# Two transformer blocks on one core: small identity products of another width and type

## The chip, the cores and the metric

The kernel runs on one core of one Trainium2 chip. The metric is the device time of one execution in microseconds; a median over runs is given, and one execution is profiled.

## The reference

Two blocks work on 256 tokens of 1024 features in fp32. The first has chunked attention beside a gated linear recurrence and a feed-forward layer; the second has four feed-forward layers, a spatial gating unit and stick-breaking attention. Each of these stages starts with a normalisation by the tokens' root mean square, and is nearly all matrix products. Cut to what matters here:

```python
def rms_norm(x, g):
    y = xf * lax.rsqrt(jnp.mean(xf * xf, axis=-1, keepdims=True) + NORM_EPS)
    return (y * g.astype(jnp.float32)).astype(x.dtype)

def swiglu(h, w_in, w_out):
    gu = h @ w_in
    gate, up = jnp.split(gu, 2, axis=-1)
    return (jax.nn.silu(gate) * up) @ w_out

def second_block(...):
    for i in range(DEPTH_2):
        x = x + FFN_RES_SCALE * swiglu(rms_norm(x, ffn_norm[i, 0]), ...)
        h = rms_norm(x, mix_norm[i])
        x = x + (chunked_sgu(h, ...) if i < N_A else stick_breaking_attention(...) @ b_w_o[j])
        x = x + FFN_RES_SCALE * swiglu(rms_norm(x, ffn_norm[i, 1]), ...)
    return rms_norm(x, final_norm)
```

## The kernel before

The program is one straight line of instructions in the order in which the code is written; each engine works off its own queue, and nothing is reordered by a planner at run time. Activations lie with features on the 128 partitions and the 256 tokens along the free axis.

**The large products.** A weight block of 1024 columns by 128 rows arrives by DMA into `raw`. ScalarE copies it to `h`, rounded to TensorE's fp32r format, and VectorE subtracts to get the remainder `l` (`prep`). The activations are split in the same way into `xh` and `xl` (or `rr`, `rr`). `mm3` makes each product from three: `h` with `xh`, `h` with `xl`, `l` with `xh`. All go through the helper `mm`, line 211, so every product in the trace has the line L211; it is told apart by the names of its tiles. Most have a weight block of 128x128 and 256 columns; a few stages (`pe_nat`, `pe_rn`) have 512 columns. fp32 and fp32r products load their own weights; a bf16 one has a separate weight load, which the order below shows as LDWEIGHTS.

**The stages.** Block 1: the columns of `w_in`, the recurrence's gates, attention, `w_o`. Then `ffn("f0")`, `ffn("f1")`, the gating unit (`sgu`), `ffn("f2")`, `ffn("f3")`, the keys and values, stick-breaking attention (`stick`), `ffn("f4")`. In a feed-forward stage the first groups of columns run on activations that aren't normalised yet; `ffn_order` then mixes groups of columns ("G") with groups of rows of the second matrix ("R").

**The normalising factors.** `stats_a` sums the squares over the partitions with two fp32 products of one column (`ones`), and GpSimd makes the factor of each token, in `rc`. `stats_b` spreads the factors over the partitions with two fp32 products of `rc` with the identity (`bcast_mm`, in the trace `ident,rc`), and ScalarE copies the result to `R`. Between the two, `nudge` issues one more product: a bf16 identity of 64 rows (`identb`) with 32 of its own columns, into a place of the bank that nobody reads.

**Where such products stand.** Sixteen in all: eight in `stats_b` (block 1, f0, f1, the gating unit, f2, f3, `stick`, f4); one behind the second broadcast of f1 (`sbb` in `block2`, line 876); one in the gating unit behind the last of `mix` (line 1066); six by `due`. `due` is set where a G group with i == 5 begins (line 772), so that `pe_a` issues the product ahead of that group's first large product, into the same place, which the large product then overwrites; this happens once in each of the five feed-forward stages, and once in block 1 behind the recurrence's last gate products (line 659).

Of the kernel before, what the change touches and what calls it, by code (L numbers as in the profile page):

```python
# [106 lines left out]
class Builder:  # L107
    def __init__(self, tc, dram, pools):
        self.tc, self.nc, self.dram = tc, tc.nc, dram
        self.cp, self.rawp, self.hlp, self.accp, self.wkp = pools  # L110
        self.ci = 0
        self.preps = 0
        self.loads = 0
        self.raw = {}
        self.hl = {}
        self.gens = []
        self.R = None
        self.rcol = None
        self.due = False

    @property
    def gi(self):
# [106 lines left out]
    def pe_a(self, h, l, xs, out, first):  # L229
        XH, XL = xs  # L230
        if first and self.due:
            self.nudge(out[:, 0:32], True)
            self.due = False
        for k in range(8):
            s = slice(k * 128, k * 128 + 128)
            self.mm3(out, h[:, s], l[:, s], XH[:, k, :], XL[:, k, :], start=(first and k == 0), stop=(k == 7))
# [52 lines left out]
            self.mm(bank[:, half, t * 128:(t + 1) * 128], col[:, t:t + 1].to_broadcast([128, 128]), self.ident,  # L289
                    start and t == 0, True)  # L290

    def nudge(self, out, start=False):

        self.mm(out, self.identb[0:64, :], self.identb[0:64, 0:32], start, True)

    def stats_a(self, pool=None, kv=False):

# [7 lines left out]
    def stats_b(self):  # L305

        self.bcast_mm(self.st, 1, self.rcol, False)
        self.nudge(self.st[:, 0, 64:96])
        self.nc.scalar.activation(self.R, self.st[:, 1, :], AF.Copy)

    def Rpair(self):
# [302 lines left out]
    def lru(self, xr, xc, rt, it, gr, gb, ga, gw):  # L614
# [4 lines left out]
        def conv(k):  # L619
            nc.scalar.activation(xc[:, k, :], xr[:, k, 0:256], AF.Identity, bias=P("conv_b", k), scale=P("conv_w", k))  # L620
            for j in range(1, 4):
                nc.vector.scalar_tensor_tensor(xc[:, k, :], xr[:, k, j:j + 256], P("conv_w", 8 * j + k), xc[:, k, :],
                                               op0=ALU.mult, op1=ALU.add)
# [30 lines left out]
        for p in range(4):  # L654
            banks = [self.acc(), self.acc()]
            for wi in range(2):
                for f in range(2):
                    self.mm(banks[wi][:, f, :], gw[:, wi * 8 + 2 * p + f, :], xc[:, 2 * p + f, :], f == 0, True)
            self.due = p == 3
            if p < 2:  # L660
                conv(2 * p + 4)
            yield
            for f in range(2):
                k = 2 * p + f
                nc.scalar.activation(rt[:, k, :], banks[0][:, f, :], AF.Sigmoid, bias=P("b_r", k))
            yield
            if p < 2:
                conv(2 * p + 5)
            yield
            for f in range(2):  # L670
                k = 2 * p + f
                nc.scalar.activation(it[:, k, :], banks[1][:, f, :], AF.Tanh, bias=self.half[:, k:k + 1], scale=0.5)
            yield
            sl = slice(2 * p, 2 * p + 2)
            nc.vector.scalar_tensor_tensor(it[:, sl, :], it[:, sl, :], 1.0, xc[:, sl, :], op0=ALU.add, op1=ALU.mult)
# [683 lines left out]
```

## Time and profile before

| what | value |
|---|---|
| median of 3 runs | 1422.33 us (1422.17 to 1423.14) |
| profiled execution, its own time | 1422.0 us |
| its span | 1420.3 us |
| TensorE (PE) busy | 1410.6 us, 99% |
| VectorE (DVE) busy | 949.8 us, 67% |
| ScalarE (ACT) busy | 735.0 us, 52% |
| granted TensorE clock, mean | 0.999 |

The span runs from the first to the last instruction; the execution's own time has 1.7 us more around it. Busy time of TensorE overlaps in the records: a product starts before the one ahead of it has ended, so the rate at which products follow is read from their starts, or from a window's length and the count in it, and not from their durations. A window of the profile lists the engine's busy time and, behind an x, the instructions that touch it; a timeline row gives start, duration, instruction, out<-in, rows\*columns of the array, and the operand's shape.

### The profile page before, as it was taken

The page shows a single profiled execution, that of the slowest core. Times are in us where ns is not written, and L with a number is a line of the kernel's source. Part 1 is how long each engine was busy: PE and PEld are TensorE (multiplying, and loading weights), DVE is VectorE, ACT ScalarE, POOL GpSimd, SP SyncE. Part 2 cuts the span into 40 slices and gives each one's busy share as a digit, 9 for nine tenths or more (in the row PEclk, how much of TensorE's full clock was granted, in tenths as well). Part 3 has the DMA queues.
Part 4 walks back from the last instruction along what each step waited for, and adds up shares of the span by engine and source line. Part 5 has one row for each costly group of instructions (what it writes and reads, how often), then busy time and mean ns, then how long its engine had stood idle before and what let it go on. Part 6 is the DMA issues. An engine that isn't in the chain of part 4 may idle for free.

```text
span 1420.3 us, 26991 instructions
## 1 busy us (share of the span) xinstructions
PE 1410.6 (99%) x11564; PEld 1368.7 (96%) x11564; DVE 949.8 (67%) x1316; ACT 735.0 (52%) x1094; POOL 24.7 (2%) x57
## 2 busy tenths in 40 slices
PE   9999999999999999999999999999999999999998
PEld 9998999999999999998999999999999998999997
DVE  6976687665567666677785665667665677656663
ACT  5686465544445445455445444446544477544442
POOL 0000000000000000000000000000000000000000
PEclk9999999999999999999999999999999999999999
DMA  8555554555544555556445554454555552445551
GB/s 299 192 198 197 176 189 154 203 195 191 179 178 149 206 182 206 203 198 223 160 156 183 186 206 179 178 188 169 208 184 211 199 179 90 161 152 197 190 187 51
DMA packets 37624, 260.31 MB, mean 183 GB/s; under 512 B 4224, under 2 KB 4608, under 8 KB 7040
## 3 DMA queue, kind: packets, MB, share of 16 engines
q1 hardware_dynamic: 36288, 253.77, 50.1%
q0 software_dynamic: 1072, 4.72, 1.0%
q8 instruction: 90, 1.47, 0.4%
q14 instruction: 30, 0.25, 0.1%
q10 hardware_dynamic: 144, 0.10, 0.0%
HBM read 257.53 MB, written 1.05 MB: 182 GB/s over the span
## 4 chain that ended last, share of the span: by engine, by line
PE 98%; DMA 0%; ACT 0%; DVE 0%; SPq 0%; issue 0%; POOLq 0%; POOL 0%
PE wk L211 62%; PE acc L211 36%; DMA raw<-w 0%; PE acc L530 0%; PE wk L530 0%; ACT sf L971 0%; ACT sd L961 0%; DVE l L164 0%; ACT h L163 0%; SPq L361 0%; SPq L352 0%; DVE sf L962 0%; POOLq L1355 0%; POOL rc L284 0%; ACT sh L1148 0%
## 5 line engine op out<-in xcount | busy, mean ns | idle before, releaser
L164 DVE TENSOR_TENSOR l<-raw,h 128x1024 fp32r<-128x1024 f32 (+1 forms) x479 | 571.3, 1220 | 241.3 <-ACT h L163 240.9
L211 PE MATMUL wk<-xh,h 128*128 128x256 f32 x2272 | 637.5, 281 | 1.4 <-ACT h L163 1.4
L211 PE MATMUL wk<-xh,l 128*128 128x256 f32 x2272 | 633.5, 279 | 0.1
L211 PE MATMUL wk<-xl,h 128*128 128x256 f32 x2272 | 633.2, 279 | 0.0
L163 ACT ACTIVATE h<-raw 128x1024 fp32r<-128x1024 f32 (+1 forms) x479 | 486.3, 1046 | 61.3 <-PE acc L211 28.0
L211 PEld LDWEIGHTS wk<-xh,h 128*128 128x128 f32 x2272 | 430.8, 190 | 4.5 <-issue 2.0
L211 PEld LDWEIGHTS wk<-xh,l 128*128 128x128 f32 x2272 | 427.7, 188 | 0.5 <-DVE l L164 0.5
L211 PEld LDWEIGHTS wk<-xl,h 128*128 128x128 f32 x2272 | 427.6, 188 | 0.5
L211 PE MATMUL acc<-rr,h 128*128 128x256 f32 x2016 | 353.5, 279 | 0.0
L211 PEld LDWEIGHTS acc<-rr,h 128*128 128x128 f32 x2016 | 306.1, 189 | 2.1 <-issue 1.9
L211 PE MATMUL acc<-rr,l 128*128 128x256 f32 x1008 | 280.4, 278 | 0.0
L211 PEld LDWEIGHTS acc<-rr,l 128*128 128x128 f32 x1008 | 189.3, 188 | 0.0
L748 ACT ACTIVATE sa<-sa 128x256 f32<-128x256 f32 x110 | 45.4, 417 | 258.5 <-DVE sa L315 258.3
L318 ACT ACTIVATE rr<-sa 128x256 fp32r<-128x256 f32 (+1 forms) x122 | 52.7, 439 | 185.3 <-DVE sa L753 128.9
L315 DVE TENSOR_TENSOR sa<-wk,rt 128x512 f32<-128x512 f32 x92 | 62.4, 687 | 72.5 <-PE wk L211 54.8
L319 DVE TENSOR_TENSOR rr<-sa,rr 128x256 fp32r<-128x256 f32 (+1 forms) x122 | 54.1, 451 | 53.4 <-ACT rr L318 53.4
L211 PE MATMUL acc<-h,rr 128*128 128x512 f32 (+1 forms) x208 | 63.1, 374 | 0.0
L211 PEld LDWEIGHTS acc<-h,rr 128*128 128x128 f32 x208 | 38.5, 188 | 6.6
L262 ACT ACTIVATE xh<-x,par 128x256 fp32r<-128x256 f32 x56 | 25.0, 501 | 29.4 <-DVE x L325 16.2
L211 PE MATMUL acc<-l,rr 128*128 128x512 f32 (+1 forms) x104 | 39.0, 375 | 0.0
L753 DVE TENSOR_TENSOR sa<-sa 128x256 f32<-128x256 f32 x88 | 37.1, 429 | 0.0
L211 PE MATMUL wk<-rr,h 128*128 128x256 f32 x192 | 33.0, 277 | 0.0
(255 smaller groups left out, 972.8 us busy)
## 6 DMA issues: line engine op xcount, KB each, us to landing
raw<-w SPq DMA_DIRECT2D x237, 1024.0 KB, 5.0
sd<-bias POOLq DMA_DIRECT2D x8, 384.0 KB, 3.4
raw<-w SPq DMA_DIRECT2D x3, 512.0 KB, 7.6
sh<-gates SPq DMA_DIRECT2D x1, 1024.0 KB, 9.1
out<-sf SPq DMA_DIRECT2D x4, 256.0 KB, 2.2
x<-x SPq DMA_DIRECT2D x3, 256.0 KB, 6.6
raw<-w SPq DMA_DIRECT2D x2, 256.0 KB, 4.9
sa<-ws POOLq DMA_DIRECT2D x1, 512.0 KB, 3.8
```

The source lines that it names most:

```text
L163: nc.scalar.activation(h[:, s], raw[:, s], AF.Copy)
L164: nc.vector.tensor_tensor(l[:, s], raw[:, s], h[:, s].bitcast(F32), op=ALU.subtract)
L211: self.nc.tensor.matmul(out, lhsT, rhs, start=start, stop=stop, skip_group_check=True)
L262: self.nc.scalar.activation(xs[0][:, k, :], src[p][:, f, :], AF.Copy, scale=self.par(*g(k)))
L315: self.nc.vector.tensor_tensor(dst, bank, self.Rpair(), op=ALU.mult)
L318: self.nc.scalar.activation(zh, src, AF.Copy)
L319: self.nc.vector.tensor_tensor(zl, src, zh.bitcast(F32), op=ALU.subtract)
L748: nc.scalar.activation(t[:, 0, :], t[:, 0, :], AF.Silu)
L753: nc.vector.tensor_tensor(t[:, 1, :], t[:, 0, :], t[:, 1, :], op=ALU.mult)
```

## The change

`nudge` takes its width from the place that it is given, and has a second form. In the eight calls of `stats_b` the bf16 product has 38 columns instead of 32. Where `due` is 2, which is the one place behind the recurrence's last gates, the product is made with the fp32 identity `ident` (64 rows, 32 columns) instead of `identb`. The other products of the kind keep their 32 columns and bf16: the five of the feed-forward stages, the one of the gating unit's `mix` and the one behind f1's second broadcast.

```diff
         XH, XL = xs
         if first and self.due:
-            self.nudge(out[:, 0:32], True)
-            self.due = False
+            self.nudge(out[:, 0:32], True, self.due == 2)
+            self.due = 0
...
-    def nudge(self, out, start=False):
-
-        self.mm(out, self.identb[0:64, :], self.identb[0:64, 0:32], start, True)
+    def nudge(self, out, start=False, wide=False):
+
+        e = self.ident if wide else self.identb
+        self.mm(out, e[0:64, :], e[0:64, 0:out.shape[-1]], start, True)
...
         self.bcast_mm(self.st, 1, self.rcol, False)
-        self.nudge(self.st[:, 0, 64:96])
+        self.nudge(self.st[:, 0, 64:102])
...
-            self.due = p == 3
+            self.due = 2 if p == 3 else 0
```

TensorE's order at the first of the eight broadcasts, before (-) and now (+); `acc` and `wk` are banks of PSUM, `xh`, `xl`, `h` the operands of the large products:

```order
 L211 MATMUL acc<-ident,rc 128x128 x2
 L211 LDWEIGHTS identb
-L211 MATMUL acc<-identb 128x32
+L211 MATMUL acc<-identb 128x38
 L211 MATMUL wk<-xh,h 128x256
 L211 MATMUL wk<-xl,h 128x256
```

Nothing moves; one product is six columns wider, and the large products follow it as before. TensorE's order behind the recurrence's last gates, at the first product of the next group of columns:

```order
 L211 MATMUL wk<-xl,h 128x256
 L211 MATMUL wk<-xh,l 128x256
-L211 LDWEIGHTS identb
-L211 MATMUL wk<-identb 128x32
+L211 MATMUL wk<-ident 128x32
 L211 MATMUL wk<-xh,h 128x256
 L211 MATMUL wk<-xl,h 128x256
```

Here the separate weight load is gone, since an fp32 product loads its own; the product stands at the same place.

## Rows read from the trace of the kernel before

**Rows 1.** The page: TensorE's busy time, and the chain that ended last, by engine.

```profile
PE 1410.6 (99%) x11564; PEld 1368.7 (96%) x11564; DVE 949.8 (67%) x1316; ACT 735.0 (52%) x1094; POOL 24.7 (2%) x57
...
PE 98%; DMA 0%; ACT 0%; DVE 0%; SPq 0%; issue 0%; POOLq 0%; POOL 0%
```

**Rows 2.** Windows of long stretches (f0, f1, f2, f3): length, PE busy (count), clock, DMA.

```profile
294.95:461.83 166.88, 166.88 (x1418) 1.00 0.51 182
483.64:630.64 147.00, 147.00 (x1298) 1.00 0.59 212
808.29:975.16 166.87, 166.87 (x1417) 1.00 0.53 191
995.86:1154.02 158.16, 158.16 (x1393) 1.00 0.55 194
```

**Rows 3.** Groups of large products within f0, then within f1: busy, mean ns.

```profile
L211 PE MATMUL wk<-xh,h 128*128 128x256 f32 x310 | 87.2, 281 | 0.0
...
L211 PE MATMUL wk<-xh,h 128*128 128x256 f32 x272 | 75.2, 276 | 0.0
```

**Rows 4.** Windows of block 1 (first stretch; behind the gates) and of f4.

```profile
29.38:46.45 17.07, 17.07 (x145) 1.00 0.34 120
73.17:107.19 34.02, 34.02 (x289) 1.00 0.55 193
107.19:129.59 22.40, 22.40 (x98) 1.00 0.50 170
1247.76:1256.35 8.59, 8.59 (x73) 1.00 0.31 96
...
1276.66:1282.15 5.49, 5.49 (x26) 1.00 0.58 191
```

**Rows 5.** Timeline of TensorE around the small products of f0 and f4.

```profile
294.62 0.28 PE L211 MATMUL acc<-rr,l 128*128 128x256 f32 x1
294.83 0.19 PE L211 MATMUL wk<-identb 64*128 64x32 bf16 x1
294.95 0.38 PE L211 MATMUL wk<-xh,h 128*128 128x256 f32 x1
295.17 0.28 PE L211 MATMUL wk<-xl,h 128*128 128x256 f32 x1
...
1265.21 0.39 PE L211 MATMUL acc<-h,rr 128*128 128x512 f32 x1
1265.53 0.19 PE L211 MATMUL wk<-identb 64*128 64x32 bf16 x1
1265.65 0.39 PE L211 MATMUL wk<-xh,h 128*128 128x256 f32 x1
```

**Rows 6.** The first large product behind the broadcast: in f0, in f3.

```profile
L211 PE MATMUL wk<-xh,h 128*128 128x256 f32 x1 | 0.4, 388 | 0.0
...
L211 PE MATMUL wk<-xh,h 128*128 128x256 f32 x1 | 0.4, 384 | 0.0
```

**Rows 7.** Timeline of TensorE: the sums ahead of f0, f1's two broadcasts.

```profile
273.62 0.28 PE L211 MATMUL wk<-xh,l 128*128 128x256 f32 x1
273.74 0.50 PE L211 MATMUL acc<-ones,sb 128*128 128x1 f32 x4
274.10 0.36 PE L211 MATMUL wk<-xh,h 128*128 128x256 f32 x1
274.30 0.28 PE L211 MATMUL wk<-xl,h 128*128 128x256 f32 x1
...
468.82 0.19 PE L211 MATMUL acc<-identb 64*128 64x32 bf16 x1
468.94 0.71 PE L211 MATMUL acc<-ident,r1c 128*128 128x128 f32 x4
469.58 0.19 PE L211 MATMUL acc<-identb 64*128 64x32 bf16 x1
469.69 0.39 PE L211 MATMUL wk<-xh,h 128*128 128x256 f32 x1
```

More of the change, by code (lines that the diff above doesn't have):

```diff
@@ L231, in pe_a @@
         if first and self.due:
-            self.nudge(out[:, 0:32], True)
-            self.due = False
+            self.nudge(out[:, 0:32], True, self.due == 2)
+            self.due = 0
         for k in range(8):
```

## The prediction

> **What bounds the kernel now.** I read the page's busy line and its chain first: TensorE is busy 99% of the span and 98% of the chain that ended last is TensorE [rows 1]. Nothing is waited for, so only what TensorE's own products take can change the time. Next I read the windows by stretch, looking at stretches with nothing in them but large products (128x256, three to each weight block). There the reader is to see that the same instructions run at two rates. In the first feed-forward f0, 1416 products take 166.88 us; in f1, 1296 products take 147.00 us [rows 2] (the count of a row includes one or two instructions that began before its window). That is 117.85 ns and 113.43 ns for a product, **4.42 ns** apart, at the same granted clock of 1.00, the 2.4 GHz level, in both. So it isn't the clock. The mean duration tells the rates apart too: 281 ns in f0, 276 ns in f1 [rows 3]. I call them the loose and the tight rhythm. f2 is loose like f0 (166.87 us), f3 is tight like f1 (158.16 us for 1392) [rows 2]. Products of 512 columns have the same pair: 22.40 us for 96 is 233.3 ns, 5.49 us for 24 is 228.8 ns [rows 4].
>
> A rhythm hardly ever changes inside such a stretch; it is set where something else passes. Three products take 340 ns in the tight rhythm and 353.3 ns in the loose one; both are whole multiples of 6.67 ns (51 and 53). Taken to the nanosecond, which the trace keeps and the printed rows round to ten, all starts of tight stretches lie at one place of a raster of 6.67 ns that runs through the whole span, and those of loose stretches at three, a third of the raster apart. So I take the rhythm to be settled by **where in the raster the first large product behind an interruption starts**; I call that its place, counted in ns from where tight stretches start theirs.
>
> **What the change does, part by part.** Eight small products get 38 columns for 32. The first question is whether that moves anything. Around such a product TensorE doesn't overlap: the small one starts 0.21 us after the last 256-column product and 0.32 us after the last 512-column one, and the next large one 0.12 us after the small one [rows 5]. So 256 more columns cost 0.11 us (0.43 ns each), and from 32 to 256 columns the step grows by 0.09 us (0.40 ns each): it is a fixed part of about 0.10 us and a stream of some 0.41 ns a column. Six more columns then start the next product **2.5 ns later**. As work that is 8 x 2.5 ns = 0.02 us, no gain and no loss; as a place in the raster it is three eighths of a period. The ends of this term are 0 (the width is hidden behind a fixed part) and 6 x 0.43 = 2.6 ns; I take 2.5, since the steps behind 32, 256 and 512 columns lie on one line.
>
> The Trainium skill, "TensorE: Matmul & The Clock Gate", section "Back-to-back issue gap", lists one and the same spacing for anything from 1 to 64 columns. By that rule 32 and 38 columns would be alike and these eight edits would do nothing; no row here shows a bf16 product of another width under 64 columns, so it isn't excluded. It is the second rival.
>
> The places, worked out from the starts to the nanosecond. At six of the eight broadcasts a large product follows at once. It starts at 3.4 in four of them (first stretch of block 1, f0, f2, f4), and all four turn loose; at 1.2 in f3 and 0.6 in the stick-breaking stage, and both turn tight. In f1 and in the gating unit another small product follows. That the four are one case shows in the rows: the first large product lasts 388 ns at each of the four, 384 ns in f3 [rows 6]. Behind the other small products, which don't change, places 0.1 to 0.5 led to the loose rhythm, 3.9 to 4.2 and 6.0 to the tight one; behind the value products of the attention, whose 64 columns also make TensorE wait, 5.7 to 6.1 led to the tight one each time. So places 0.1 to 0.5 and about 2.9 to 3.4 lead into the loose rhythm, all others that were seen into the tight one. The change puts the four from 3.4 to **5.9**: tight.
>
> That settles most of it. Behind the broadcast in f0 come 120 products and then the small one that `due` sets, which keeps 32 columns: from a tight stretch it led into a tight one in f1 and f3, from a loose one into a loose one in f0 and f2. So f0 gains on 120 + 1416 = 1536 products: 1536 x 4.42 ns = 6.79 us. f2 has the same counts: 6.79 us. Block 1's 144 products [rows 4] give 144 x 4.42 = 0.64 us, f4's 72 give 0.32 us.
>
> f3 is tight now only because it comes out of a loose f2: its places are shifted against f0's from the start. With f2 tight it enters as f0 does now, its broadcast at 3.4 + 2.5 = 5.9 too: tight again, 0 us. f1 has two broadcasts in a row, the first now with 38 columns and the second still with 32 [rows 7], and it too comes out of a tight stretch for the first time; carried through its steps its entry falls near 6.1 or 4.7, both tight, so 0 us, but this is the least certain step. The gating unit is tight behind its broadcast; two rounds of small products stand between, so I leave it so (0 us; at worst 132 wide and 144 large products turn loose, +1.2 us). The stick-breaking stage moves from 0.6 to 3.1, loose, for 36 products until other work interrupts: +0.16 us. Two brief stretches (48 at the gates, 24 in f1) should turn loose, since what comes before them is tight: 72 x 4.42 = +0.32 us.
>
> The product at the gates becomes fp32: its separate weight load goes, and it makes more than one pass. Bound from below: two fp32 products of one column, without a change of rows, put 0.68 us between the starts of the large products around them [rows 7], where two plain steps would take 0.23; so 0.22 us each. The bf16 one now costs 0.32 (0.21, 0.12 and 0.22 to the second large product [rows 5], less the 0.23 of two plain steps), by 0.10 more: -0.10 us. From above: the fp32 broadcast behind a 64-row product takes 0.21 us from its first half to its second (0.64 us to the next small product, less two halves of 0.11 and a wait of 0.21) [rows 7], all of it extra: +0.21 us. It has 64 rows as well, so I lean to the upper end: +0.1. What it does to the rhythm counts more. The 288 products and 96 wide ones behind it are loose now [rows 4]. The places it can reach spread over most of the raster, of which about two thirds are tight; I take tight: 288 x 4.42 = 1.27 and 96 x 4.5 = 0.43, together 1.70 us.
>
> Sum: -6.79 - 6.79 - 0.64 - 0.32 - 1.70 + 0.16 + 0.32 + 0.10 + 0.02 = **-15.6 us**. The profiled execution took 1422.0 us, so 1406.4; the median of the runs is 0.3 us higher, so **1406.8 us**. Covers: TensorE in f0 and f2 would want its weights 4% earlier, and f1 and f3, with the same plan, already run so without a wait.
>
> **The rivals.**
> 1. f1 tips. Its second broadcast lands in a loose place, and with it the whole of f1: 1416 x 4.42 = 6.3 us given back: 1413.1. For it: two small products in a row, and an order of entry that the trace doesn't hold. Against it: both ways of carrying the steps through end in tight places.
> 2. The width is hidden, and only the gates' product acts: -1.6 us if it gives the tight rhythm, +0.1 if not: 1420.7 to 1422.4. For it speaks that the step behind the small product can't be seen at another width; against it the line through 32, 256 and 512 columns.
> 3. Slower. The width moves the entry by 2.5 ns, but 5.9 is a loose place for these. Then f0 and f2 stay loose, f3 still comes out of a loose f2, and its entry goes from 1.2 to 3.7, which lies between 3.4 (loose) and 3.9 (tight). If that is loose, f3's 120 + 1392 products lose 1512 x 4.42 = 6.7 us: 1427 to 1429. It decides from a place of under about 3.65. Against it: every entry seen between 5.7 and 6.1 turned tight.
> 4. As rival 3, but f3 stays tight: about 1421.
>
> **How the numbers follow.** Forecast 0.47 (1405 to 1409, by whether the gates turn tight), rival 1 0.16, rival 2 0.20, rival 3 0.11, rival 4 0.06. A measurement of this kernel can tell about 0.2% (2.8 us) from no change. Faster by more: 0.47 + 0.16 = 0.63; within it: 0.20 + 0.06 = 0.26; slower: 0.11. The range runs from 1405.0 to 1422.6, which leaves out rival 3 and the tails of the others; the forecast's own range is 1405 to 1409.
>
> **What would show it.** In the changed kernel's trace: the step from the small product to the next large one at the broadcasts stays 0.12 us, but the mean duration of f0's and f2's large products falls from 281 to 276 ns, and their main stretches take about 160.6 us; f1's and f3's stay at 276 ns. If f0 still shows 281 ns while the first large product behind its broadcast lasts other than 388 ns, the width moved the entry and I had the wrong map; if it still lasts 388 ns, the width is hidden. If f1 or f3 shows 281 ns, rival 1 or 3. The forecast is wrong as a whole if the rhythm isn't settled at these entries, which would show as changes of rhythm in the middle of a stretch.

## The result, and the profile after

The changed kernel takes 1407.41 us (1407.05 to 1407.65 in 4 runs), the kernel before 1422.74 us beside it (1422.17 to 1424.44 in 4 runs): a ratio of 0.9892, with a 95% interval from 0.9877 to 0.9907, so 15.3 us less. The forecast of 1406.8 us was 0.6 us off. The profiled execution took 1407.16 us, its span 1405.4 us against 1420.3 us.

The page's line on busy time, and the chain by engine, answer to [rows 1]:

```profile
PE 1395.3 (99%) x11565; PEld 1353.6 (96%) x11565; DVE 949.4 (68%) x1316; ACT 735.0 (52%) x1094; POOL 24.8 (2%) x57
...
PE 98%; DMA 1%; ACT 0%; SPq 0%; DVE 0%; issue 0%; POOLq 0%; POOL 0%
```

TensorE has one instruction more, is as full as before, and is done 15 us earlier. VectorE and ScalarE do the same work in the same time. So the products follow one another more closely, and the windows of the stretches say where. Columns: window and its length, PE busy (instructions that touch it), granted clock, DMA share, GB/s. In this order: block 1's first stretch, behind the gates (256-wide and 512-wide), the main stretches of f0, f1, f2, f3, the stick-breaking stage's, f4's:

```profile
29.99:46.44 16.45, 16.45 (x145) 1.00 0.32 121
73.56:106.33 32.77, 32.77 (x289) 1.00 0.58 198
106.33:128.30 21.97, 21.97 (x98) 1.00 0.52 174
293.15:453.75 160.60, 160.60 (x1417) 1.00 0.53 190
475.66:622.66 147.00, 147.00 (x1297) 1.00 0.59 212
799.79:960.39 160.60, 160.60 (x1417) 1.00 0.55 198
981.09:1139.25 158.16, 158.16 (x1393) 1.00 0.54 194
...
1144.60:1149.04 4.44, 4.44 (x37) 1.00 0.64 240
...
1233.22:1241.50 8.28, 8.28 (x73) 1.00 0.28 83
```

Against [rows 2, 4]: f0 and f2 went from 166.88 and 166.87 to 160.60 us each, the same 1416 products at the same clock; f1 (147.00) and f3 (158.16) are where they were. The 120 products ahead of f0's main stretch, first in the kernel before, then in the changed one:

```profile
280.49:294.83 14.34, 14.34 (x121) 1.00 0.27 89
```

```profile
279.21:293.03 13.82, 13.82 (x121) 1.00 0.27 82
```

The groups of products within f0's main stretch and, under the dots, the product behind its broadcast (busy us, mean ns) answer to [rows 3] and [rows 6]:

```profile
L211 PE MATMUL wk<-xh,h 128*128 128x256 f32 x312 | 86.2, 276 | 0.0
...
L211 PE MATMUL wk<-xh,h 128*128 128x256 f32 x1 | 0.4, 394 | 0.0
```

f0 now has the mean of 276 ns that f1 had, and its first large product lasts 394 ns, which neither the 388 of the old f0 nor the 384 of f3 is: it starts at another place in the raster. The timeline of TensorE at the two kinds of changed product (start, duration, instruction, rows\*columns, operand), at f0's broadcast and at the gates:

```profile
278.56 0.61 PE L211 MATMUL acc<-ident,rc 128*128 128x128 f32 x4
279.09 0.19 PE L211 MATMUL acc<-identb 64*128 64x38 bf16 x1
279.21 0.39 PE L211 MATMUL wk<-xh,h 128*128 128x256 f32 x1
...
73.02 0.28 PE L211 MATMUL wk<-xh,l 128*128 128x256 f32 x1
73.23 0.41 PE L211 MATMUL wk<-ident 64*128 64x32 f32 x2
73.56 0.39 PE L211 MATMUL wk<-xh,h 128*128 128x256 f32 x1
```

The step behind the 38-column product is still 0.12 us. The fp32 one is two passes, and lies 0.54 us between the large products around it where the bf16 one took 0.33 (0.21 and 0.12 in [rows 5]).

Places in the raster are worked out from starts to the nanosecond, finer than the rows print; those below were found as the prediction's were. The starts of the tight stretches drift against an exact 6.67 ns by about 1.6 ns in a millisecond, which is taken out, and a start is a whole nanosecond, so a place is good to about half a nanosecond. In the changed kernel the entries of block 1, f0, f1, f2, f3 and f4 stand at 5.9, 6.3, 5.9, 6.1, 5.4 and 6.1, all tight; the stick-breaking stage's at 3.0, loose; the one at the gates at 2.6, tight.

### The profile page after: what moved, and what is told of

Its sections match the earlier page's. It is cut to its first block, busy times and chain, and to the rows that moved or that the text cites. A ratio compares the mean times of both kernels' runs of the same rounds, so it can differ in the third digit from the quotient of the medians.

```text
span 1405.4 us, 26993 instructions
## 1 busy us (share of the span) xinstructions
PE 1395.3 (99%) x11565; PEld 1353.6 (96%) x11565; DVE 949.4 (68%) x1316; ACT 735.0 (52%) x1094; POOL 24.8 (2%) x57
## 3 DMA queue, kind: packets, MB, share of 16 engines
q8 instruction: 90, 1.47, 0.4%
## 4 chain that ended last, share of the span: by engine, by line
PE 98%; DMA 1%; ACT 0%; SPq 0%; DVE 0%; issue 0%; POOLq 0%; POOL 0%
PE wk L211 62%; PE acc L211 36%; DMA raw<-w 1%; PE acc L531 0%; PE wk L531 0%; ACT sf L972 0%; ACT sd L962 0%; SPq L362 0%; DVE l L164 0%; ACT h L163 0%; SPq L351 0%; SPq L353 0%; DVE sf L963 0%; POOLq L1356 0%; POOL rc L284 0%
## 5 line engine op out<-in xcount | busy, mean ns | idle before, releaser
L211 PE MATMUL acc<-rr,h 128*128 128x256 f32 x2016 | 348.9, 277 | 0.0
```

What stands on the lines that cost most here:

```text
L211: self.nc.tensor.matmul(out, lhsT, rhs, start=start, stop=stop, skip_group_check=True)
```

## The experiments

The kernels differ from the changed one only in the small products, in their widths, types, rows or number; since nobody reads these, every kernel computes the whole. The eight widths are in a list in the order of the program: block 1, f0, f1, gating unit, f2, f3, stick-breaking stage, f4. The kernel before took 1422.3 to 1423.0 us beside them. Diffs are against the changed kernel.

**One half alone.** e1 keeps the 38 columns and takes the fp32 product at the gates back:

```
-            self.due = 2 if p == 3 else 0
+            self.due = p == 3
```

> The changed kernel with the old bf16 product of 32 columns at the gates, so only the width at the eight broadcasts is changed. Raster theory: the gates' 288 products and 96 wide ones stay loose, all else as in the changed kernel: 1407.4 + 1.7 of rhythm - 0.2 of the fp32 product's own cost = 1408.9 us, f0 and f2 at 276 ns mean. Rival (the widths bring little and the fp32 product shifts everything behind it into the tight rhythm): about 1421 us, f0 and f2 at 281 ns.

It took 1408.15 us (1408.02 to 1408.28), a ratio of 0.9899 (0.9879 to 0.9919). e2 keeps the fp32 product and gives the eight broadcasts 32 columns again:

```
+WIDTHS = (32, 32, 32, 32, 32, 32, 32, 32)
-        self.nudge(self.st[:, 0, 64:102])
+        self.nudge(self.st[:, 0, 64:64 + WIDTHS[self.nth]])
```

> The kernel before with the fp32 product at the gates alone; the broadcasts keep 32 columns. Raster theory: the 288 and the 96 wide products behind the gates turn tight, nothing behind block 1 changes, since the stretches between reset the place: -1.5 us, 1421.1 us; f0 and f2 stay at 281 ns. Rival (as above): about 1409 us.

It took 1421.15 us (1420.35 to 1421.60), 0.9991 (0.9981 to 1.0001). The windows behind the gates and of f0, first in e1, then in e2 (f2's is as f0's in both):

```profile
72.79:106.81 34.02, 34.02 (x289) 1.00 0.59 197
294.05:454.65 160.60, 160.60 (x1417) 1.00 0.53 190
```

```profile
73.28:106.05 32.77, 32.77 (x290) 1.00 0.59 199
293.38:460.26 166.88, 166.88 (x1417) 1.00 0.51 182
```

The two halves act apart: the width turns f0 and f2 tight and leaves the gates loose, the fp32 product turns the gates alone. Of the 15.3 us, about 14 belong to the width and a little over 1 to the product at the gates. The second share rests on the window, since the interval of e2's time just includes no change. In e2's profiled execution block 1's first stretch ran tight too, entered at 2.1 with the instructions of before; nothing that stands behind it can have done that, so even this place differs from one execution to another.

**Other widths.** If six columns help because TensorE does something better with 38, then 40, 44 and 48 should help as well. If all that counts is where the next product starts, then the width acts modulo the raster: 16 columns more at 0.41 ns are 6.6 ns, about one whole period of 6.67 ns, and should do nothing.

```
+WIDTHS = (48, 48, 48, 48, 48, 48, 48, 48)
```

> The kernel before with 48 columns at the eight broadcasts. 16 columns more are 16 x 0.417 = 6.67 ns, one whole period of the raster. Raster theory: every place is as before, so f0 and f2 are loose (281 ns) again and the first large product behind the broadcast lasts 388 ns: 1422.6 us. Rival (a wider product gives TensorE more time and any width from some point on is good): 1408.9 us, f0 and f2 at 276 ns.

Like e4 to e6 below, e3 is otherwise the kernel before, with the bf16 product at the gates. It took 1422.84 us, a ratio of 1.0002 (0.9992 to 1.0013). With 40 and 44 columns:

> The kernel before with 40 columns at the eight broadcasts: 8 more, 3.33 ns, half a period. Raster theory: the four loose ones go from 3.4 to 6.7, next to 0.1 (loose) and past 6.3 (tight): I expect loose, f0 and f2 at 281 ns, f1 and f3 tight, 1422.6 us, though 38 columns gave 14 us. Rival (every width from 38 on is good except by whole periods of 48): 1408.5 us, 276 ns.

> The kernel before with 44 columns at the eight broadcasts: 12 more, 5.0 ns. Raster theory: from 3.4 to 8.4, which is 1.7, tight (f1's entry now and f3's were 1.2 to 2.1): f0 to f4 all at 276 ns, 1408.5 us. Rival (38 fits for a reason of its own, such as where its columns end): 1422.6 us or another time.

40 columns (e5) took 1422.35 us, 1.0000 (0.9989 to 1.0010); 44 (e6) took 1408.76 us (1408.38 to 1409.15), 0.9904 (0.9885 to 0.9924). The windows of f0 with 48, with 40 (and f3's under it) and with 44 columns (f2's is as f0's, and f1's main stretch is tight, 147.00 us, in all three):

```profile
295.26:462.14 166.88, 166.88 (x1418) 1.00 0.51 182
```

```profile
295.41:462.29 166.88, 166.88 (x1417) 1.00 0.50 182
...
996.32:1154.48 158.16, 158.16 (x1393) 1.00 0.55 194
```

```profile
294.61:455.21 160.60, 160.60 (x1417) 1.00 0.53 190
```

So 32, 40 and 48 columns leave f0 and f2 loose, 38 and 44 make them tight. No monotone effect of the width gives that order. The three loose widths are also the multiples of 8, but that isn't the cause either: with 40 columns f3's broadcast, at 4.2, leads into the tight rhythm (its main stretch is above), and with 38 the stick-breaking stage, at 3.0, is loose. f0's entry stands at 3.4 with 32 columns, 6.3 with 38, 0.5 with 40, 1.3 with 44 and 3.3 with 48, back where 32 columns put it. The step from the small product to the next large one grows along: 115 to 116 ns with 32 columns, 118 to 119 with 38, 119 to 120 with 40, 120 to 122 with 44, 122 to 123 with 48. That is about 0.4 ns for each column. A timeline row prints ten nanoseconds, and there the step is 0.12 us with 38 columns and with 48 (280.68 to 280.80 us in e3's f0).

The reader should see that 13 us hang on a difference that no printed row of a timeline shows; what shows it is the mean duration and the length of the stretch behind.

**One stage alone.** The prediction says that f3 was tight before only because it came out of a loose f2. e4 gives only f2's broadcast 38 columns:

```
+WIDTHS = (32, 32, 32, 32, 38, 32, 32, 32)
```

> The kernel before with 38 columns at f2's broadcast alone. Raster theory: f2 turns tight, -6.8 us; f3 then enters as f0 does, its broadcast of 32 columns at place 3.4, and turns loose, +6.7 us: 1422.5 us, with f2 at 276 ns and f3 at 281 ns. Rival (each stage is settled by its own broadcast alone): f3 stays tight, 1415.8 us.

It took 1421.90 us (1421.42 to 1422.90), 0.9997 (0.9986 to 1.0007). The windows of f0, f2 and f3, and a group of f3's large products:

```profile
295.05:461.93 166.88, 166.88 (x1418) 1.00 0.51 182
807.87:968.47 160.60, 160.60 (x1417) 1.00 0.55 198
989.69:1153.57 163.88, 163.88 (x1393) 1.00 0.52 187
```

```profile
L215 PE MATMUL wk<-xh,h 128*128 128x256 f32 x272 | 76.5, 281 | 0.0
```

f2 gains its 6.3 us, and f3, whose own instructions are those of before, loses 5.7 of it in its main stretch (158.16 in [rows 2]) and another 0.5 in the 120 products ahead. Its entry stands at 2.9, where 32 columns behind a tight stage put it. The stages are a chain, and a gain in one can be taken back by the next without anything changing there.

**The wait of the small product, and its worth.** In [rows 5] the small product starts 0.21 us after the last large one. I took the change of rows from 128 to 64 and back to be the cause. e9 is e1 with 128 rows in the eight broadcasts' products:

```
+        r = 64 if out.shape[-1] == 32 else 128
-        self.mm(out, e[0:64, :], e[0:64, 0:out.shape[-1]], start, True)
+        self.mm(out, e[0:r, :], e[0:r, 0:out.shape[-1]], start, True)
```

> As the 38 columns at the broadcasts alone (bf16 product of 32 at the gates), but with all 128 rows of the identity in those eight products instead of 64. Theory: the wait around the small product comes from its other number of rows; with 128 rows it overlaps as the large ones do, the 0.21 us step ahead of it and the 0.12 us behind it go, each costs about 0.11 instead of 0.32 us, and the place of the next large product is then not set by 2.5 ns of width; which rhythm follows isn't known, loose being likelier, as behind other small products of 128 rows. Rival (the wait comes from the change between bf16 and fp32): steps and time as with 64 rows, 1408.2 us.

It took 1413.31 us (1412.98 to 1413.36), 0.9929 (0.9907 to 0.9952). Its timeline at f0's broadcast, and the windows of f0, f1 and f2:

```profile
279.87 0.61 PE L215 MATMUL acc<-ident,rc 128*128 128x128 f32 x4
280.31 0.18 PE L215 MATMUL acc<-identb 128*128 128x38 bf16 x1
280.34 0.36 PE L215 MATMUL wk<-xh,h 128*128 128x256 f32 x1
```

```profile
294.25:454.85 160.60, 160.60 (x1418) 1.00 0.53 190
477.05:629.77 152.72, 152.72 (x1297) 1.00 0.57 204
806.71:967.31 160.60, 160.60 (x1417) 1.00 0.55 197
```

The wait is gone: from the first identity product to the large one 0.47 us, against 0.65 with 64 rows (278.56 to 279.21 above). That the wait comes from the number of rows is shown. My guess that such entries are likelier loose was wrong: of the six with a large product right behind, the stick-breaking stage's turned loose (at 4.7), the other five tight (at 6.2 to 6.6 and 0.1 to 0.4). f1 turned loose as well, but behind its second small product, which keeps 32 columns and 64 rows (at 6.2). f1 alone costs 5.7 us in its main stretch and 0.5 ahead of it, more than the eight shorter steps bring.

e10 is the kernel before without the eight products:

```
-        self.nudge(self.st[:, 0, 64:102])
...
-            self.due = 2 if p == 3 else 0
+            self.due = p == 3
```

> The kernel before without the eight small products at the broadcasts; the other eight stay. Raster theory: behind a plain fp32 product of 128 rows every stretch in the trace of the kernel before but one turned loose, so f0 to f3 start loose and the second small product finds them at places that stay loose: 1422.4 + 13.5 (f1, f3) - 8 x 0.32 = about 1433 us, f0 to f3 at 281 ns. Rival (the small product isn't needed, the broadcast itself will do): f1 and f3 stay tight, about 1420 us.

It took 1420.53 us (1419.82 to 1420.88), 0.9981 (0.9970 to 0.9993). The windows of f0 and f3 (f2's is as f0's, 166.88 us, f1's 147.00):

```profile
294.64:461.52 166.88, 166.88 (x1417) 1.00 0.51 183
...
994.30:1152.46 158.16, 158.16 (x1393) 1.00 0.55 194
```

The 1433 us that I thought likelier was wrong; the rhythms are those of [rows 2] in all four stages. With 32 columns the eight products bought no rhythm and cost some 2.5 us in all, about 0.3 us each. They earn their place only at a width that puts the next product right.

**Fewer of them.** Where a stretch is entered tight, the product that `due` sets inside it has nothing to mend. e7 drops it in the five feed-forward stages, gives the one at the gates 38 columns in bf16 instead of fp32, and the stick-breaking stage its 32 again:

```
+WIDTHS = (38, 38, 38, 38, 38, 38, 32, 38)
-            self.nudge(out[:, 0:32], True, self.due == 2)
+            self.nudge(out[:, 0:max(32, self.due)], True)
-            self.due = 2 if p == 3 else 0
+            self.due = 38 if p == 3 else 0
-                self.due = i == 5
```

> The changed kernel without the five small products that follow in the feed-forward stages 120 products behind the broadcast, with a bf16 product of 38 columns at the gates, and 32 columns at the broadcast of the stick-breaking stage. Raster theory: a stretch that is tight already stays tight without them, so five times 0.32 us are saved; the bf16 product at the gates lands at 2.6 as the fp32 one did and is 0.2 us cheaper; the 36 products of the stick-breaking stage and some behind them turn tight, -0.3 us: 1407.4 - 1.6 - 0.2 - 0.3 = 1405.3 us. Rival (each feed-forward stage needs its second small product to be tight): five stages at 281 ns, about 1434 us.

It took 1405.07 us (1404.51 to 1406.24), 0.9880 (0.9865 to 0.9894). The changed kernel itself, on the same chip, beside it:

> The changed kernel as it is, beside the one above on the same chip: 1407.4 us by both.

1407.51 us (1407.04 to 1408.36), 0.9897 (0.9880 to 0.9913). The windows of e7 behind the gates, and of f0 and f1 from the broadcast to the stage's end:

```profile
73.25:106.02 32.77, 32.77 (x289) 1.00 0.59 200
```

```profile
278.90:453.11 174.21, 174.21 (x1538) 1.00 0.51 182
461.07:621.68 160.61, 160.61 (x1418) 1.00 0.57 206
```

The changed kernel needs 174.54 us for f0 (279.21 to 453.75 in the windows above) and 160.94 for f1; each stage saves 0.33 us, which is what one such product costs. e7's kernel was run again on another chip (e12):

> The lean kernel as it was, beside the one above on the same chip: 1405.1 us by both.

It took 1405.04 us (1404.84 to 1406.10), 0.9879 (0.9863 to 0.9896). It is the best steady version: e7 stands 2.4 us under e8 beside it, and the times of the two don't overlap.

e11 adds 128 rows where e9 stayed tight (block 1, f0, f2, f3, f4), to save the waits too:

```
+ROWS = (128, 128, 64, 64, 128, 128, 64, 128)
-        self.nudge(self.st[:, 0, 64:102])
+        self.nudge(self.st[:, 0, 64:64 + WIDTHS[self.nth]], rows=ROWS[self.nth])
```

> The lean kernel with 128 rows of the identity instead of 64 in the small products of five broadcasts (block 1, f0, f2, f3, f4), where 128 rows were seen to lead into the tight rhythm; f1, the gating unit and the stick-breaking stage keep 64. Raster theory: all stages enter as in the run with 128 rows, stay tight, and each of the five costs 0.2 us less: 1405.1 - 1.0 = 1404.1 us. Rival (the places move, since the stretches ahead differ): one of the stages turns loose, about 1411 us.

Its four runs went from 1403.20 to 1410.13 us, with a median of 1404.40, 0.9881 (0.9860 to 0.9901). The longest is the profiled one. Its windows at the end of the stick-breaking stage, cut in two, and of f4, and under them those of e12:

```profile
1198.98:1201.82 2.84, 2.84 (x27) 1.00 0.92 365
1202.07:1226.09 24.02, 24.02 (x204) 1.00 0.47 171
1250.31:1390.52 140.21, 140.21 (x1009) 1.00 0.47 166
```

```profile
1198.53:1201.46 2.93, 2.93 (x27) 1.00 0.95 370
1201.62:1224.77 23.15, 23.15 (x206) 1.00 0.48 170
1248.89:1385.56 136.67, 136.67 (x1010) 1.00 0.47 170
```

In that execution 203 products at the end of the stick-breaking stage and all of f4's 256-wide products ran loose: 0.87 and 3.54 us of the 5.0 between the two spans. The two executions do not part once and for all. Behind TensorE's wait for ScalarE in the stick-breaking stage (0.47 us in both) twelve large products are loose in e11 and tight in e12, both entered at 3.7; but the first 25 of the windows above are tight in e11 and loose in e12. Both change at the cut, and there TensorE waits again, for VectorE, e11 first:

```profile
1201.60 0.42 DVE L1167 TENSOR_TENSOR rr<-acc,rr 128x256 fp32r<-128x256 f32 x1
```

```profile
1201.15 0.42 DVE L1166 TENSOR_TENSOR rr<-acc,rr 128x256 fp32r<-128x256 f32 x1
```

The next large product starts 0.05 us after the end of that instruction in both, at 1202.07 and 1201.62 us. The profile lists no idle time there, because the product ahead still counts as busy; only the step tells, 0.26 and 0.17 us where 0.11 to 0.12 is usual. The place was 3.4 in e11 and 2.4 in e12. The same happens in one and the same program. The changed kernel's first trace and e8's, behind this wait:

```profile
1203.33:1226.45 23.12, 23.12 (x204) 1.00 0.45 166
```

```profile
1202.88:1226.90 24.02, 24.02 (x204) 1.00 0.48 172
```

The places were 4.7 and 3.6. So the loose end of the stick-breaking stage is no doing of e11's 128 rows. What e11 lacks is something that mends it: its f4 was entered at 3.8, behind 128 rows, and without the product that `due` set nothing in f4 moves the rhythm again; e8's f4, entered behind 64 rows at 4.6, was tight. The other three executions of e11 have no trace, so that their f4 was tight is only inferred from their times. Whether 64 rows at f4 alone would make this version steady wasn't tried.

## Why the prediction was right, point by point

**What bounds the kernel.** Two rhythms at one clock, set by the place of the first large product behind an interruption: e3, e5 and e6 show it as a cause, since the same edit in other sizes acts modulo 6.67 ns. The main stretches of f0, f1 and f2 kept one rhythm in every kernel. f3's did not quite: in its last 90 products or so, where some have their operands in the other order (`h,rr`), the rhythm changes back and forth, in the kernel before as in all others. The prediction had named such changes as a sign against it; these are the same before and after and take no part in the gain.

**The map was too broad.** The prediction says that all places but 0.1 to 0.5 and 2.9 to 3.4 led into the tight rhythm. That holds behind its small products. Behind the sums (`ones,sb`) ahead of f0 and of f2, in the same trace, a large product at about 4.7 led into the loose one. It didn't hurt, since the broadcasts that the change moves are all of the first kind.

**The width moves the next product by 0.41 ns a column.** Right; 38 columns moved the entries by 2 to 3 ns, 48 by a whole period. That it was enough was in part luck: f0 came in at 6.3, not at 5.9, and at 6.3 others turned loose, f4 with 40 columns among them. The margin is small: two columns more turned all four entries loose in e5. The Trainium skill, "TensorE: Matmul & The Clock Gate", section "Back-to-back issue gap", gives one spacing for 1 to 64 columns; the rival built on it is excluded here by e1, e5, e6 and e3, where the step grows from 116 to 122 ns between 32 and 48 columns. The Trainium skill, "TensorE: Matmul & The Clock Gate", section "Step-by-step: what each phase is for", says of the weight load that its time goes by the columns and that the row count K doesn't matter. The trace agrees: the 32 loads of the bf16 identity in the kernel before, half with 64 rows and half with 128, took 92 to 98 ns. What e9 shows is a wait of the products: another row count than that of the neighbours costs 0.18 us at a broadcast.

**f0 and f2, 6.79 us each.** Measured: 13.82 us for the 120 products and 160.60 for the rest, against 14.34 and 166.88: 0.52 + 6.28 = 6.80 us each.

**Block 1 and f4, 0.64 and 0.32.** 17.07 to 16.45 is 0.62; f4's 72 products take 8.28 us, where 8.59 in [rows 4] gives 0.31.

**f1 and f3, nothing.** Right, f1 at 5.9 where I had 6.1 or 4.7, f3 at 5.4 where I had 5.9. That f3 would have lost 6 us at 32 columns is what e4 shows (5.7 + 0.5; the 6.7 of rival 3 counts the last 90 products or so as well, which run in both rhythms anyway); the width is right in a chain, not one by one. Rivals 1, 3 and 4 are excluded by the windows of f0 to f3, rival 2 by e1.

**The gates.** The rhythm term was right: 34.02 to 32.77 and 22.40 to 21.97, together 1.68 us where I had 1.70. It was a choice by likelihood, since the place couldn't be worked out from the rows, and that it came true was luck: the entry stands at 2.6 here and at 2.8 in e2 and e8, next to the 2.9 from which others turned loose. The product's own cost was **mis-sized**: +0.22 us (0.54 to 0.33 at its step, the step behind it equal), where I took +0.10; the upper bound of 0.21, from an fp32 product's second pass, was the right one.

**The stick-breaking stage.** 36 products loose, 4.30 to 4.44 us, as forecast. Not counted was that three more short stretches of twelve stay loose behind them. The windows after:

```profile
1154.05:1155.55 1.50, 1.50 (x15) 1.00 0.39 164
1156.72:1158.23 1.51, 1.51 (x15) 1.00 0.00 0
1160.20:1161.72 1.52, 1.52 (x14) 1.00 0.04 11
```

In the kernel before they took 1.46, 1.47 and 1.49 us (1168.67 to 1170.13, 1171.31 to 1172.78, 1174.76 to 1176.25), so that is another 0.11 us. (In e8 the stretch of 203 behind the wait for VectorE was loose too, 0.9 us; the forecast left this scatter out.) The **brief stretches** at the gates (48) and in f1 (24) turned loose as forecast:

```profile
55.36:61.20 5.84, 5.84 (x50) 1.00 0.75 236
457.39:460.30 2.91, 2.91 (x26) 1.00 0.25 104
```

5.84 against 5.64 (55.38 to 61.02 before), and 2.91 against 2.81: +0.3, where I had 0.32.

**The sum.** With the measured terms: -13.60 - 0.62 - 0.31 - 1.68 + 0.14 + 0.11 + 0.30 + 0.22 + 0.02 = -15.4. The two spans differ by 14.9. The missing 0.5 lies ahead of all of it: block 1's first stretch began at 29.99 us where it was 29.38 in [rows 4]. In the other kernels' profiles, which share that part but for the small product at its end, it began between 29.43 and 31.19, so this is scatter of the start and no effect of the change; it nearly vanishes in the medians, which differ by 15.3. The recorded sum has a slip of 0.1 at its end: 1406.4 and 0.3 make 1406.7.

**Why "the width is hidden" deserved less than 0.20.** Its only support was a step that couldn't be seen at another width, while three widths of the same step lay on one line. The range, wide because of it and rival 1, could have been narrower.

## What to carry to other kernels

When two stretches of the same instructions differ by a few per cent at the same clock, with nothing waited for, count their products and compare the time for one: TensorE can settle into more than one rhythm, and what settled it here is where the first product behind an interruption starts, to the nanosecond, and what kind of product stands ahead of it. A small product of a chosen width can then shift that start, but its effect is periodic and passes on to the next stages, so all of them are carried through together, and the whole is timed at several widths. Where a rhythm hangs on a moment that another engine sets, leave something behind it that sets the rhythm anew, or the time will scatter.

## What the runs showed of the hardware

- The raster of 6.67 ns shows in every trace, for the fp32r products that load their own weights. Behind a product that makes TensorE wait (64 rows or columns, or a wait for another engine; the first large product then lasts 383 to 395 ns), some 470 entries in the fourteen traces give one map: places 0.8 to 2.8 and 3.9 to 6.1 led to 113.4 ns a product, those at 3.1 to 3.6 and 6.4 to 0.3 to 117.8; at the borders (0.4 to 0.5, 2.9 to 3.0, 3.7 to 3.8, 6.2 to 6.3) both were seen. The map in the prediction had the second loose zone at 0.1 to 0.5 only; with 40 columns entries at 6.4 (block 1) and 6.6 (f2) turned loose too.
- Behind a product of 128 rows that the large one overlaps (it then lasts 364 to 369 ns) some 370 entries give another map: 6.1 to 0.4 and 1.2 to 2.0 tight, 2.0 to 3.0 and 3.8 to 5.5 loose. The entries of e9 and e10 at the broadcasts fit it. Why the raster exists, and why the map depends on what stands ahead, isn't settled by these runs.
- A bf16 product with 64 rows between products of 128 rows costs some 0.3 us, most of it waiting: with 128 rows the step ahead falls from 0.21 to 0.11 us, and the one behind from 0.12 to 0.03 us.
- A wait for another engine lets two executions of the same program part ways: behind a wait for VectorE that costs 0.05 to 0.15 us and shows as no idle time, the same 203 products took 23.12 and 24.02 us in two traces of the changed kernel. In e11, where nothing behind it sets the rhythm anew, f4 cost 3.5 us more as well, 50 to 190 us later.
